# Two mixers of a hybrid diffusion backbone: later gate tiles traced while the pooling is awaited, the decays of both directions in one piece, and other filling steps

## The chip, the cores and the metric

The kernel runs on one core of one Trainium2 chip, as one launch. The metric is the device time of that launch in microseconds (us). The engines that matter here are TensorE (PE, matrix products; its weight loads are shown as PEld), VectorE (DVE), ScalarE (ACT, activation functions and copies), and SyncE (SP), which issues the DMAs. All tensors are fp32 in HBM.

## The reference

Two layers (DEPTH = 2) act on 256 latent tokens and 256 context tokens of width 1024. Each layer is a half-step SwiGLU FFN, a token mixer, and another half-step FFN, all with adaLN shift, scale and gate. The mixer is the part that matters here:

```python
cq, ckv, kr, pz, gq, gk, gv, ga, gr, gates = split_cols(u @ w_in)
q, k, v = mla_project(cq, ckv, kr, ...)      # low-rank q and kv, RMS-norm per head, rotary part
o_a = blocked_attend(q, k_all, v_all)        # 8 heads; latent queries see context and latent keys
o_p = multiscale_pool(pz, w_pool, pool_scale)  # 4 channel groups, windows 2/4/8/16
og  = gla_bidir(qg, kg, vg, la, s_f, s_b)    # gated linear attention, forward and backward scan
o_g = gla_output(og, gr, g_gla_o)            # RMS-norm, times silu(gr)
g = sigmoid(gates)                           # 3 x 1024 gate channels
m = g[0] * (o_a @ w_branch[0]) + g[1] * (o_p @ w_branch[1]) + g[2] * (o_g @ w_branch[2])
y = m @ w_out
```

In GLA every direction has its own decay: `log_sigmoid` of a low-rank product, summed over chunks of 64 tokens, and its exponentials scale queries and keys. The context tokens of the second layer need no mixer output, so mixer 1 computes queries, gates and outputs for the 256 latent tokens alone, and mixer 0 for all 512. Only the latent stream is returned.

## The kernel before

Activations lie transposed, channels on the 128 partitions, tokens along the row (512: latent, then context). Every product with a weight is three fp32r matmuls (mm3, lines 219 to 221) of a high and a low part of both operands. Weights come in 512 KB pieces through SP's queue into four raw buffers. ACT copies out the high part (whi, traced at line 185 by act) and DVE subtracts (wlo, line 197). The class Weights loads and cuts ahead, in the order in which the trace asks for the pieces, as far as the raw buffers and 20 slots of 128x512 (in the mixers) reach. In all there are 71 such slots in SBUF and 8 PSUM banks of 128x512.

A planner schedules what the Python code traces: each engine has one queue, and its order is in the main that of the trace, with single instructions moved by the planner's own times. So the order of tracing is the tuning knob. A mixer is written as generators that are advanced in turn (mixer, lines 665 to 735):

- attend: the set-up of keys and queries (step a0: squares; a1: norms of the compressed q and kv; four steps k: two heads' keys each, with key_tail, the mean and the scaling, one step behind; then the value products, the last key_tail; four steps q: two heads' queries each; qs: the queries' scale rq), then per block scores (s) and turn and value products (t). Scores, row maximum (mx), exponential (p), sum and division run over PE, DVE and ACT, and the turned p goes through PSUM (pt, pT).
- gla: two pairs of heads. gla_prepare makes the logits (line 1157), for each direction the decays (lines 1159 to 1181, Abs, Exp and Ln on ACT, a scan on DVE) with a step g1, and turns the end-scaled keys (ket, line 1186, step g2). gla_pair makes A (line 1207, g3), the state increments ds and the state chain st (lines 1225 to 1233, g3), the outputs o per head (lines 1244 to 1258, g4), and their turn ot (g5).
- pool: for each of the four groups, windowed sums on DVE (line 1109), 1 + POOL[l] steps of waiting, and the product with w_pool, whose result goes to self.op.
- filler: all the remaining PE work, in pieces of half a weight tile (twelve matmuls; tile_of). In mixer 0: four pooling inputs, then a wait for self.op, branch 1 (per four channels: gate tiles 8 to 15 where they are missing, sigmoids, four branch products), the GLA inputs, four output gates (gr), a wait for the attention's outputs self.oa, branch 0, four gate tiles, a wait for GLA, branch 2. In mixer 1 the GLA inputs come first.

In mixer 0 attend and gla run one behind the other, in mixer 1 in turn. After every step of either the pool is advanced by one step, and the filler gets the credit that FILL[l] names for that step; one whole credit is one filler step. A filler step spent while the filler waits for self.op or self.oa emits nothing. What is left of the filler is emitted when both chains have ended. act keeps the order of all users of an activation table: sigmoid and silu need another table than exp and ln, so each change of kind is a table load (line 181) that lies between its users in ACT's queue.

Of the kernel before, what the change touches and what calls it, by code (L numbers as in the profile page):

```python
# [15 lines left out]
P = 128  # L16
# [23 lines left out]
ROOM_0, ROOM_1, LAST = 8, 36, 4  # L40
S0, S1, S2 = 7, 3, 3

FILL = (dict(a0=1.5, a1=2, k=1.5, q=0, qs=2, s=0.5, t=1, g1=3, g2=3.5, g3=1.5, g4=1.5, g5=0, w=0.5),
        dict(a0=1, a1=1.5, k=2, q=3.5, qs=0.5, s=2, t=2, g1=0.5, g2=0, g3=0.5, g4=1, g5=0.5, w=0.5))
POOL = (0, 1)
EDGE = {(1, 17): (1, 2), (0, 17): (0, 2)}
LATE = 100
ADA = dict(up=(1.5, 1.25, 1, 0), down=(1, 1, 1, 0), mix=(12, 10), late=(8, 26), pre=(2, 1, 1, 0), premix=(0, 0))
# [89 lines left out]
class Net:  # L138
# [611 lines left out]
    def filler(self, adas):  # L750


        n, u, l = self.n, self.u, self.l
        w_in = self.a["w_in"][l]
        left = [adas]

        def tile_of(c0, m):
            unit = self.cols(w_in, 0, KD, c0)
            o = self.ps("fill")
            for k in range(KD):  # L760
                self.mm3(o[:, 0:m], unit.block(k), (u[k][0][:, 0:m], u[k][1][:, 0:m]), k == 0, k == KD - 1)
                if k == 3:
                    yield 1
            self.w.done(unit)
            left[0] -= 1
            if 0 <= left[0] < ADA["mix"][l]:
                self.adas(1)
            self.got = o

        def kept(c0, m, name):  # L770
            yield from tile_of(c0, m)
            t = self.slot(name=name, n=m)
            self.act(out=t[:, 0:m], in_=self.got[:, 0:m], func=AF.Copy)
            self.got = t

        def gate(j):
            yield from kept(2496 + j * P, n, "gate")
            self.gates[j] = self.got
            yield 1

        def branch(i, x):
            wb = self.a["w_branch"][l, i]
            for d0 in range(0, KD, 4):
                dcs = range(d0, d0 + 4)
                for dc in dcs:
                    if 8 * i + dc not in self.gates:
                        yield from gate(8 * i + dc)
                for dc in dcs:
                    s = self.gates[8 * i + dc]
                    self.act(out=s[:, 0:n], in_=s[:, 0:n], func=AF.Sigmoid)  # L790
                for dc in dcs:
                    s = self.gates.pop(8 * i + dc)
                    (o,) = self.dense([self.cols(wb, 0, 4, dc * P)], x, n)
                    self.nc.vector.tensor_tensor(out=s[:, 0:n], in0=s[:, 0:n], in1=o[:, 0:n], op=ALU.mult)
                    if dc in self.m:
                        self.nc.vector.tensor_tensor(out=s[:, 0:n], in0=s[:, 0:n], in1=self.m[dc][:, 0:n], op=ALU.add)
                    self.m[dc] = s if i < 2 else self.parts(s[:, 0:n], n)
                    yield 1

        def pools():  # L800
            for g in range(4):
                yield from tile_of(416 + g * P, n)
                self.pz[g] = self.got
                yield 1

        def glas():
            for c0, m, to in ((1184, T, self.gk), (928, n, self.gq)):
                for c in range(2):
                    yield from kept(c0 + c * P, m, "gqk")
                    to.append(self.got)  # L810
                    yield 1
            out = [self.ps("gv") for _ in range(4)]
            for q in range(4):
                unit = self.cols(w_in, 2 * q, 2, 1440, T)
                for kk in range(2):
                    k = 2 * q + kk
                    for tt, o in enumerate(out):
                        x = tuple(t[:, tt * P:(tt + 1) * P] for t in u[k])
                        self.mm3(o, x, unit.block(kk, T), k == 0, k == KD - 1)
                    if kk == 0:  # L820
                        yield 1
                self.w.done(unit)
                if q < 3:
                    yield 1
            for o in out:
                t = self.slot(name="gv")
                self.act(out=t, in_=o, func=AF.Copy)
                self.gv.append(t)
            yield 1

        if not self.full:
            yield from glas()
        yield from pools()
        while len(self.op) < 4:
            yield 1
        yield from branch(1, self.op)
        self.op.clear()
        if self.full:
            yield from glas()
        for g in range(4):  # L840
            yield from kept(1984 + g * P, n, "gr")
            self.gr.append(self.got)
            yield 1
        while len(self.oa) < 4:
            yield 1
        oa = [self.parts(t[:, 0:n], n) for t in self.oa]
        self.oa.clear()
        yield from branch(0, oa)
        oa.clear()
        for dc in range(4):  # L850
            yield from gate(16 + dc)
        while len(self.on) < 4:
            yield 1
        og = []
        for h in range(4):
            self.act(out=self.gr[h][:, 0:n], in_=self.gr[h][:, 0:n], func=AF.Silu)
        for h in range(4):
            t = self.on[h]
            self.nc.vector.tensor_tensor(out=t[:, 0:n], in0=t[:, 0:n], in1=self.gr[h][:, 0:n], op=ALU.mult)
            og.append(self.parts(t[:, 0:n], n))  # L860
        self.on.clear()
        self.gr.clear()
        yield from branch(2, og)


    def attend(self):
        nc, l, n, a = self.nc, self.l, self.n, self.a
# [23 lines left out]
        t = self.slot(name="ckv")  # L891
# [8 lines left out]
        for j, p in enumerate((pq0, pq1)):  # L900
            t = self.slot(name="cq")
# [28 lines left out]
        def key_tail(j, ps, sq):  # L930
            ms = self.ps("kms")
            nc.tensor.matmul(ms, cst[:, C_1H:C_1H + P], sq, start=True, stop=True)
            r = sq
            self.rstd_from(ms, r)
            for x in range(2):
                o = slice(64 * x, 64 * x + 64)
                t = self.slot(name="k")
                nc.vector.scalar_tensor_tensor(out=t[0:64], in0=ps[o], scalar=vec[o, V_KN2:V_KN2 + 1], in1=r[o], op0=ALU.mult, op1=ALU.mult)
                nc.vector.tensor_tensor(out=t[64:128], in0=krr[o], in1=r[o], op=ALU.mult)
                keys[2 * j + x] = t  # L940
# [11 lines left out]
        v = []  # L952
        for tt in range(4):
# [3 lines left out]
            t = self.slot(name="v")  # L957
            self.act(out=t, in_=ps, func=AF.Copy)
            v.append(t)
        self.w.done(wkv)  # L960
        key_tail(*pend)


        wq = []
# [17 lines left out]
        q = []  # L982
# [158 lines left out]
    def gla_prepare(self, c, ready):  # L1141
# [16 lines left out]
        for d, ps in enumerate(logits):  # L1158
            bias = vec[:, V_BA + 2 * d + c:V_BA + 2 * d + c + 1]
            e = self.slot(name="e")  # L1160
            self.act(out=e, in_=ps, func=AF.Abs, bias=bias)
            self.act(out=e, in_=e, func=AF.Exp, scale=-1.0)
            self.act(out=e, in_=e, func=AF.Ln, bias=1.0)
            la = self.slot(name="la")
            nc.vector.tensor_scalar(out=la, in0=ps, scalar1=bias, scalar2=0.0, op0=ALU.add, op1=ALU.min)
            nc.vector.tensor_tensor(out=la, in0=la, in1=e, op=ALU.subtract)
            b = self.slot(name="b")
            if d == 0:
                nc.vector.tensor_tensor_scan(out=b, data0=rst, data1=la, initial=0.0, op0=ALU.mult, op1=ALU.add)
            else:  # L1170
                nc.vector.tensor_tensor_scan(out=b[:, ::-1], data0=rst, data1=la[:, ::-1], initial=0.0, op0=ALU.mult, op1=ALU.add)
            end = 63 if d == 0 else 0
            nc.vector.tensor_tensor(out=chunk(la), in0=chunk(b)[:, :, end:end + 1].to_broadcast([P, 8, 64]), in1=chunk(b), op=ALU.subtract)
            self.act(out=la, in_=la, func=AF.Exp, scale=1.0 / 16)
            nc.vector.tensor_tensor(out=la, in0=gk, in1=la, op=ALU.mult)
            ket.append(la)
            self.act(out=e, in_=b, func=AF.Exp, scale=1.0 / 16)
            self.act(out=b[:, 0:n], in_=b[:, 0:n], func=AF.Exp, scale=-1.0 / 16)
            nc.vector.scalar_tensor_tensor(out=qt[d][:, 0:n], in0=gq[:, 0:n], scalar=0.125, in1=e[:, 0:n], op0=ALU.mult, op1=ALU.mult)
            nc.vector.tensor_tensor(out=kt[d][:, 0:n], in0=gk[:, 0:n], in1=b[:, 0:n], op=ALU.mult)  # L1180
            nc.vector.tensor_copy(dec[:, d, :], chunk(e)[:, :, end])
            yield "g1"
        for d in range(2):
            pt = self.ps("ket")
            for tt in range(4):
# [209 lines left out]
```

## Time and profile before

| | |
|---|---|
| median of 3 runs | 2154.8 us (2153.69 to 2155.99) |
| the profiled execution's own time | 2152.27 us |
| its span in the profile | 2150.5 us |
| mean granted PE clock | 0.983 |
| HBM traffic | 287.44 MB read, 134 GB/s over the span |
| mixer 0, from its norm to its last output tile | about 421 to 897 us |
| mixer 1, likewise | about 1644 to 1946 us |

A row of a timeline reads: start, duration (us), engine, line, operation, output <- inputs, form, count, and in brackets the idle time of that engine just before and what ended it. A matmul's duration includes its pipeline, so back-to-back matmuls start closer together than they last. A stretch's clock of 0.58 means that PE got 58% of its full clock on average. Names are the kernel's tile names; fill is a filler tile in PSUM, ps any dense product, uhi and ulo the normed input.

### The profile page before, as it was taken

To read this page: it belongs to the slowest core of one execution; us is meant where nothing else is said; L and a number is where in the kernel's file an instruction comes from. 1 tells how busy PE (TensorE), PEld (TensorE's weight loads), DVE (VectorE), ACT (ScalarE), POOL (GpSimd) and SP (SyncE) were. 2 spreads that over 40 slices of the span, in tenths; PEclk is the share of its full clock that TensorE was granted. 3 is DMA by queue.
4 is the path that set the end of the run, shared out by engine and by line. 5 is a ranking of instruction groups with operands and counts; after the bars stand their busy time and mean duration, and the time that the engine had idled before them with its cause. 6 is when DMAs were issued, how large, how long until landed. Compare 5 with 4: busy or idle time off the path is not lost.

```text
span 2150.5 us, 29894 instructions
## 1 busy us (share of the span) xinstructions
PE 2084.2 (97%) x11388; PEld 1752.5 (81%) x11388; DVE 1453.7 (68%) x2870; ACT 882.3 (41%) x1797; POOL 2.0 (0%) x10
## 2 busy tenths in 40 slices
PE   7999999898999999999999989999999998999999
PEld 4888778786777887888888888888888777998997
DVE  4577877867586665666876785767544687666564
ACT  5232223455344555433223342323343656665552
POOL 0000000000000000000000000000000000000000
PEclk9999999999999999999999999999999989999999
DMA  9355554514432223445555453546442332566663
GB/s 318 100 152 157 172 166 134 160 39 127 118 108 69 79 69 98 119 124 152 164 164 161 135 149 102 151 141 186 137 115 59 96 101 80 142 163 192 181 197 127
DMA packets 431071, 290.43 MB, mean 135 GB/s; under 512 B 16464, under 2 KB 386768, under 8 KB 430928
## 3 DMA queue, kind: packets, MB, share of 16 engines
q1 hardware_dynamic: 430016, 287.09, 46.6%
q8 instruction: 89, 1.46, 0.3%
q10 hardware_dynamic: 912, 1.44, 0.2%
q14 instruction: 54, 0.44, 0.1%
HBM read 287.44 MB, written 1.05 MB: 134 GB/s over the span
## 4 chain that ended last, share of the span: by engine, by line
PE 74%; DVE 11%; DMA 9%; ACT 3%; issue 2%; ACTq 0%; SPq 0%; DVEq 0%
PE ps L219 17%; PE ps L220 17%; PE ps L221 17%; DMA raw<-in_ffn_w_dram 9%; PE fill L219 4%; PE fill L221 4%; PE fill L220 4%; DVE wlo L197 4%; DVE adaacc L358 2%; ACT whi L185 2%; PE sc L1031 1%; PE av L1067 1%; PE ada L327 1%; PE pt L1049 1%; PE gv L219 1%
## 5 line engine op out<-in xcount | busy, mean ns | idle before, releaser
L197 DVE TENSOR_TENSOR wlo<-raw,whi 128x512 fp32r<-128x512 f32 (+3 forms) x912 | 531.3, 619 | 290.0 <-ACT whi L185 279.6
L185 ACT ACTIVATE whi<-raw 128x512 fp32r<-128x512 f32 (+3 forms) x912 | 471.9, 568 | 521.5 <-DMA raw<-in_ffn_w_dram 469.8
L219 PE MATMUL ps<-uhi,whi 128*128 128x512 f32 (+1 forms) x1620 | 564.3, 350 | 8.7 <-ACT uhi L185 5.1
L221 PE MATMUL ps<-uhi,wlo 128*128 128x512 f32 (+1 forms) x1620 | 561.8, 348 | 1.1 <-DVE wlo L197 1.1
L220 PE MATMUL ps<-ulo,whi 128*128 128x512 f32 (+1 forms) x1620 | 562.3, 348 | 0.0
L219 PEld LDWEIGHTS ps<-uhi,whi 128*128 128x128 f32 x1620 | 308.0, 191 | 53.7 <-ACT uhi L185 8.7
L221 PEld LDWEIGHTS ps<-uhi,wlo 128*128 128x128 f32 x1620 | 308.8, 191 | 41.3 <-DVE wlo L197 3.6
L220 PEld LDWEIGHTS ps<-ulo,whi 128*128 128x128 f32 x1620 | 309.3, 191 | 37.9 <-DVE ulo L475 0.6
L358 DVE SCALAR_TENSOR_TENSOR adaacc<-raw,csil,adaacc 128x512 f32<-128x512 f32 x420 | 294.6, 744 | 1.6 <-DMA raw<-in_w_ada_dram 0.8
L219 PE MATMUL ps<-hi,whi 128*128 128x512 f32 (+1 forms) x738 | 272.8, 371 | 6.9 <-DVE h L501 5.4
L221 PE MATMUL ps<-hi,wlo 128*128 128x512 f32 (+1 forms) x738 | 272.0, 369 | 0.2 <-DVE wlo L197 0.2
L220 PE MATMUL ps<-lo,whi 128*128 128x512 f32 (+1 forms) x738 | 271.5, 368 | 0.0
L219 PE MATMUL fill<-uhi,whi 128*128 128x512 f32 (+1 forms) x576 | 203.9, 354 | 0.0
L221 PE MATMUL fill<-uhi,wlo 128*128 128x512 f32 (+1 forms) x576 | 195.9, 340 | 0.0
L220 PE MATMUL fill<-ulo,whi 128*128 128x512 f32 (+1 forms) x576 | 195.4, 339 | 0.0
L219 PEld LDWEIGHTS ps<-hi,whi 128*128 128x128 f32 x738 | 141.2, 191 | 29.8 <-DVE h L501 5.8
L221 PEld LDWEIGHTS ps<-hi,wlo 128*128 128x128 f32 x738 | 141.2, 191 | 23.2 <-DVE wlo L197 0.6
L220 PEld LDWEIGHTS ps<-lo,whi 128*128 128x128 f32 x738 | 141.3, 192 | 22.4 <-DVE lo L197 0.2
L570 DVE TENSOR_TENSOR silu<-silu,ps 128x512 f32<-128x512 f32 (+1 forms) x88 | 54.2, 616 | 133.7 <-ACT silu L185 79.3
L185 ACT ACTIVATE silu<-ps 128x512 f32<-128x512 f32 (+1 forms) x88 | 47.4, 539 | 195.4 <-PE ps L221 195.1
L219 PEld LDWEIGHTS fill<-uhi,whi 128*128 128x128 f32 x576 | 109.3, 190 | 21.7 <-issue 10.6
L220 PEld LDWEIGHTS fill<-ulo,whi 128*128 128x128 f32 x576 | 109.4, 190 | 13.5 <-issue 2.4
(265 smaller groups left out, 2192.0 us busy)
## 6 DMA issues: line engine op xcount, KB each, us to landing
raw<-in_ffn_w_dram SPq DMA_DIRECT2D x198, 512.0 KB, 4.4
raw<-in_w_ada_dram SPq DMA_DIRECT2D x128, 512.0 KB, 3.8
raw<-in_w_in_dram SPq DMA_DIRECT2D x86, 512.0 KB, 4.4
raw<-in_ffn_w_dram SPq DMA_DIRECT2D x48, 384.0 KB, 3.9
raw<-in_ffn_w_dram SPq DMA_DIRECT2D x48, 320.0 KB, 3.2
raw<-in_w_branch_dram SPq DMA_DIRECT2D x48, 256.0 KB, 2.9
ada<-in_w_ada_dram SPq DMA_DIRECT2D x32, 256.0 KB, 5.4
raw<-in_w_out_dram SPq DMA_DIRECT2D x16, 512.0 KB, 5.0
```

The lines of the kernel that those rows point to most:

```text
L185: i = self.nc.scalar.activation(**k)
L197: self.nc.vector.tensor_tensor(out=lo, in0=src, in1=f32hi, op=ALU.subtract)
L219: mm(out, wh, xh, start=start, stop=False)
L220: mm(out, wh, xl, start=False, stop=False)
L221: mm(out, wl, xh, start=False, stop=stop)
L327: nc.tensor.matmul(ps[32 * g:32 * g + 32, :], self.csil[:, k, :], r[i], start=(k < 4), stop=(k >= 4))
L358: nc.vector.scalar_tensor_tensor(out=acc[s], in0=r[i], scalar=c, in1=acc[s], op0=ALU.mult, op1=ALU.add)
L570: nc.vector.tensor_tensor(out=s[:, 0:n], in0=s[:, 0:n], in1=p3[:, 0:n], op=ALU.mult)
L1031: nc.tensor.matmul(sc[:, 0:nk], q[h][:, tt * P:(tt + 1) * P], keys[h][:, k0:T], start=True, stop=True)
L1049: nc.tensor.transpose(pt[:, (2 * x + j) * P:(2 * x + j + 1) * P], ps_[j][:, (kt + x) * P:(kt + x + 1) * P], self.ident)
L1067: nc.tensor.matmul(av[0][64 * x:64 * x + 64, s * NL:(s + 1) * NL], v[2 * s + kt][:, (h + x) * 64:(h + x) * 64 + 64], pts[x][kt // 2][:, (k ...
```

## The change

Four edits, all in the order of the trace:

- The filler, while self.op is awaited, traces up to GATES[l] later tiles (2 in mixer 0; 12 in mixer 1) where it traced nothing: first the gates 8 to 15, then the output gates gr. What is made there is left out where it stood.
- attend has two new steps "v", before and after the last key_tail, with one credit each in mixer 0 and none in mixer 1 (where each step also gives gla and the pool their turn).
- gla_prepare traces the decays of both directions in one piece and then yields g1 twice.
- Credits change: in mixer 0 q from 0 to 0.5; in mixer 1 qs from 0.5 to 1.5, g1 from 0.5 to 1.5, g3 from 0.5 to 1. POOL[0] goes from 0 to 1, so the pool of mixer 0 waits one more step between a group's sums and its product.

```diff
--- before.py
+++ after.py
@@ -40,9 +40,10 @@
 ROOM_0, ROOM_1, LAST = 8, 36, 4
 S0, S1, S2 = 7, 3, 3
 
-FILL = (dict(a0=1.5, a1=2, k=1.5, q=0, qs=2, s=0.5, t=1, g1=3, g2=3.5, g3=1.5, g4=1.5, g5=0, w=0.5),
-        dict(a0=1, a1=1.5, k=2, q=3.5, qs=0.5, s=2, t=2, g1=0.5, g2=0, g3=0.5, g4=1, g5=0.5, w=0.5))
-POOL = (0, 1)
+FILL = (dict(a0=1.5, a1=2, k=1.5, v=1, q=0.5, qs=2, s=0.5, t=1, g1=3, g2=3.5, g3=1.5, g4=1.5, g5=0, w=0.5),
+        dict(a0=1, a1=1.5, k=2, v=0, q=3.5, qs=1.5, s=2, t=2, g1=1.5, g2=0, g3=1, g4=1, g5=0.5, w=0.5))
+POOL = (1, 1)
+GATES = (2, 12)
 EDGE = {(1, 17): (1, 2), (0, 17): (0, 2)}
 LATE = 100
 ADA = dict(up=(1.5, 1.25, 1, 0), down=(1, 1, 1, 0), mix=(12, 10), late=(8, 26), pre=(2, 1, 1, 0), premix=(0, 0))
@@ -773,6 +774,11 @@
             self.act(out=t[:, 0:m], in_=self.got[:, 0:m], func=AF.Copy)
             self.got = t
 
+        def out_gate(g):
+            yield from kept(1984 + g * P, n, "gr")
+            self.gr.append(self.got)
+            yield 1
+
         def gate(j):
             yield from kept(2496 + j * P, n, "gate")
             self.gates[j] = self.got
@@ -831,16 +837,21 @@
         if not self.full:
             yield from glas()
         yield from pools()
+
+        later = [gate(8 + j) for j in range(8)] + [out_gate(g) for g in range(4)]
+        spare = GATES[l]
         while len(self.op) < 4:
-            yield 1
+            if spare:
+                spare -= 1
+                yield from later.pop(0)
+            else:
+                yield 1
         yield from branch(1, self.op)
         self.op.clear()
         if self.full:
             yield from glas()
-        for g in range(4):
-            yield from kept(1984 + g * P, n, "gr")
-            self.gr.append(self.got)
-            yield 1
+        for g in range(len(self.gr), 4):
+            yield from out_gate(g)
         while len(self.oa) < 4:
             yield 1
         oa = [self.parts(t[:, 0:n], n) for t in self.oa]
@@ -958,7 +969,9 @@
             self.act(out=t, in_=ps, func=AF.Copy)
             v.append(t)
         self.w.done(wkv)
+        yield "v"
         key_tail(*pend)
+        yield "v"
 
 
         wq = []
@@ -1179,7 +1192,8 @@
             nc.vector.scalar_tensor_tensor(out=qt[d][:, 0:n], in0=gq[:, 0:n], scalar=0.125, in1=e[:, 0:n], op0=ALU.mult, op1=ALU.mult)
             nc.vector.tensor_tensor(out=kt[d][:, 0:n], in0=gk[:, 0:n], in1=b[:, 0:n], op=ALU.mult)
             nc.vector.tensor_copy(dec[:, d, :], chunk(e)[:, :, end])
-            yield "g1"
+        yield "g1"
+        yield "g1"
         for d in range(2):
             pt = self.ps("ket")
             for tt in range(4):
```

## The prediction

> **What bounds the kernel now.** I read the page first, then the busy time by stretches, the waits of TensorE (PE) in the two mixers, and last the timelines around the longest waits.
>
> ```profile
> span 2150.5 us, 29894 instructions
> PE 2084.2 (97%) x11388; PEld 1752.5 (81%) x11388; DVE 1453.7 (68%) x2870; ACT 882.3 (41%) x1797; POOL 2.0 (0%) x10
> ```
>
> PE is busy in 97% of the span, so a change that moves work without removing any can win only where PE stands idle or runs below its full clock. The stretches show where that is. Columns: stretch, its length, busy time of PE, PE's weight loads, DVE, ACT and POOL with instruction counts, the granted PE clock, DMA share, GB/s.
>
> ```profile
> 480.00:520.00 40.00, 33.04 (x140) 24.02 (x139) 31.37 (x62) 24.44 (x52) 0.00 (x0) 0.87 0.33 92
> 1718.00:1853.70 135.70, 122.36 (x960) 100.72 (x959) 104.86 (x248) 83.80 (x184) 0.00 (x0) 0.91 0.33 87
> 1718.00:1744.80 26.80, 26.60 (x241) 22.08 (x240) 24.18 (x60) 18.61 (x44) 0.00 (x0) 1.00 0.36 94
> 1744.80:1761.10 16.30, 11.24 (x50) 6.92 (x50) 12.96 (x41) 5.04 (x14) 0.00 (x0) 0.58 0.16 48
> 1785.90:1798.60 12.70, 4.62 (x23) 3.49 (x24) 9.70 (x21) 9.25 (x18) 0.00 (x0) 0.60 0.21 61
> 1853.70:1917.30 63.60, 63.60 (x529) 63.52 (x530) 42.04 (x81) 41.63 (x91) 0.00 (x0) 1.00 0.69 183
> ```
>
> The first row is the query stage of mixer 0, the second the whole attention and GLA stage of mixer 1 with its two bad places below it. The last row is the rest of mixer 1's filler, made when both chains have ended: PE is full there. So any filler tile made earlier, in an idle place, shortens that stretch one for one. The waits (waiting line, what it waited for, total us, times, longest), the first four from mixer 0, the others from mixer 1:
>
> ```profile
> PE pool L219 <- ACT hi L185: 3.8, 1, 3.8
> PE kms L932 <- DVE k L938: 2.4, 1, 2.4
> PE q L219 <- ACT sqk L185: 0.8, 1, 0.8
> ...
> PE o L1248 <- DVE st L1233: 0.5, 1, 0.5
> ...
> PE ket L1186 <- DVE la L1175: 8.3, 2, 8.1
> PE pool L219 <- ACT hilo L185: 2.3, 2, 1.8
> PE o L1244 <- DVE op L1128: 1.7, 1, 1.7
> PE o L1248 <- DVE st L1233: 1.1, 1, 1.1
> ```
>
> **The most the change can win.** Idle time plus the part of the busy time that the clock withheld. Mixer 0: 40.00 - 33.04 = 6.96 us idle, which is the first three waits (7.0); the clock took (1 - 0.87) x 33.04 = 4.3. Together 11.3. Mixer 1, around 1745: 16.30 - 11.24 = 5.06 idle, and 0.42 x 11.24 = 4.7 by the clock; around 1786: 12.70 - 4.62 = 8.08 idle, and 0.40 x 4.62 = 1.9. Together 19.7. The cap is 31.0 us.
>
> **The change, part by part.** No arithmetic is added or removed: two yields are new, and the order changes. I counted the steps of both mixers by the code, since each yield gives the filler its credit. A filler step is twelve matmuls:
>
> ```profile
> 447.37:450.12 2.75, 2.75 (x15) 2.26 (x14) 0.49 (x1) 2.22 (x5) 0.00 (x0) 1.00 0.00 0
> ...
> 1717.48 0.28 PE L219 MATMUL fill<-uhi,whi 128*128 128x256 f32 x1
> ...
> 1718.80 0.28 PE L221 MATMUL fill<-uhi,wlo 128*128 128x256 f32 x1
> ```
>
> The first row is one step of mixer 0 (2.75 us). The other two start the first and the twelfth matmul of a step in mixer 1: 1.32 us for eleven gaps, so 0.12 us each and 1.44 us a step.
>
> *Decays in one piece (mixer 1).* The 8.1 us wait has a plain cause in the timelines of ACT and PE:
>
> ```profile
> 1781.66 1.28 ACT L181 ACT_TABLE_LOAD   x1
> ...
> 1783.45 1.33 ACT L185 ACTIVATE gate<-gate 128x256 f32<-128x256 f32 x4
> ...
> 1785.31 1.28 ACT L181 ACT_TABLE_LOAD   x1
> ...
> 1787.14 0.67 ACT L185 ACTIVATE e<-logit,vec 128x512 f32<-128x512 f32 x1
> ```
>
> ```profile
> 1719.01 1.13 PE L1157 MATMUL logit<-ga,wa 32*128 32x512 f32 x4
> ...
> 1734.67 0.55 PE L1186 MATMUL ket<-cst,la 128*128 128x128 f32 x3 [0.20 <-DVE la L1175]
> ...
> 1774.44 1.13 PE L1157 MATMUL logit<-ga,wa 32*128 32x512 f32 x4
> ...
> 1794.02 1.11 PE L1186 MATMUL ket<-cst,la 128*128 128x128 f32 x4 [8.09 <-DVE la L1175]
> ```
>
> The second fence has the two pairs of GLA heads, each from its logits to its ket. In the second both logits were there at 1775.6, but a yield lies between the two directions, the filler put four gate sigmoids into it, and act() keeps the order of table users. So the second direction began at 1787.14, behind two table loads. After the change both decays are traced before any filler, and by my count no sigmoid falls between them in either pair. Seven filler steps, a score block and a turn lie between logits and ket of the second pair, about 12.5 us, where both decays took 14.5 us in the first pair (1720.1 to 1734.7), with a filler step between them. I expect this wait to go, or to shrink to 0 to 2 us.
>
> *Gates while the pooling is awaited (mixer 1).* Twelve filler steps are empty now between the pooling's first group and its fourth, in exactly the 1745 stretch. Afterwards none is: gates 8 to 15 fill them, and the pooling, decay and state steps get 1.4 to 5.8 us of cover each. The extra weight cuts meet a DVE that is 90% busy just before (24.18 of 26.80). The state updates after ds still need DVE. I leave 3 us of wait here (bounds 0 and the 5.06 idle of now).
>
> *What is late next.* The filler is finite. Four output gates and the eight gates are made early, then the filler waits for all of the attention's output: four empty steps now, 24 afterwards. From the second pair's A products on (scores 4 to 7, both halves of o, the last turns) there is no cover at all. PE work of that stage, from the same stage of before, which ran full; the second and third rows are its filler tiles and branch products:
>
> ```profile
> 1799.55:1853.69 54.14, 54.14 (x463) 46.02 (x461) 37.70 (x87) 32.27 (x69) 0.00 (x0) 1.00 0.33 89
> 1799.55:1853.69 54.14, 26.37 (x193) 23.89 (x193) 3.02 (x8) 1.00 0.33 89
> 1799.55:1853.69 54.14, 6.82 (x48) 5.98 (x48) 1.59 (x4) 0.00 (x0) 1.00 0.33 89
> ```
>
> 54.14 - 240 x 0.12 = 25.3 us, in 18 pieces of 1.4 us on average. Its DVE and ACT work:
>
> ```profile
> L197 DVE TENSOR_TENSOR wlo<-raw,whi 128x512 fp32r<-128x512 f32 x19 | 12.5, 686 | 7.4 <-ACT whi L185 7.3
> L1033 DVE TENSOR_REDUCE mx<-sc 128x1 f32<-128x512 f32 x8 | 5.5, 689 | 2.8 <-PE sc L1031 2.8
> L1039 DVE TENSOR_SCALAR p<-p,mx 128x512 f32<-128x512 f32 x8 | 3.9, 487 | 0.3
> L1233 DVE SCALAR_TENSOR_TENSOR st<-st,dec,ds 128x128 f32<-128x128 f32 x12 | 3.9, 344 | 0.2
> L1054 DVE COPY pT<-pt 128x512 f32<-128x512 f32 x5 | 3.4, 685 | 1.5 <-PE pt L1049 1.5
> ...
> L185 ACT ACTIVATE p<-sc,mx,scal 128x512 f32<-128x512 f32 x16 | 12.4, 774 | 10.7 <-DVE mx L1035 10.7
> ```
>
> DVE without the weight cuts: 37.70 - 12.5 = 25.2, as much as PE, so latency decides. The o products need fourteen state updates (14 x 0.34 = 4.8) behind two score maxima (1.4): 6.2, against a turn and the first o products, some 2 us: 4.2 short. A score block's softmax takes 0.69 + 0.77 + 0.49 and some small ones, 2.3 for its first half and about 3.5 for both. The last two turns have two pieces of cover each (2.8): 0.7 short twice, and the last copy (0.69) before the last products. Sum 6.3. A wait of that size is followed by a low clock: two such drops cost 4.3 us in mixer 0, so 2.1 for one. I take 8.4. Bounds: 0 if the planner puts gate tiles from behind into the gaps (it does move single matmuls, as the pooling product amid the ds shows), and at the other end the 1745 stretch, which ran like operations without cover: 0.58 x 11.24 = 6.5 us of full-clock work in 16.30, a factor 2.5, +38 us here.
>
> ```profile
> 1739.86 0.39 PE L219 MATMUL pool<-hilo,whi 128*128 128x256 f32 x1
> 1740.17 0.65 PE L1225 MATMUL ds<-gv,ket 64*64 64x128 f32 x10
> ```
>
> The clock has a page in the Trainium skill, "TensorE: Matmul & The Clock Gate", section "HAM oscillation — how this bites in real kernels": only idle gaps beyond some 3.4 us cost clock. By that rule the late stage's short gaps would keep it, save perhaps the 4.2, and its loss would be 6.3 rather than 8.4. The 1745 stretch disagrees: its gaps are 1.7, 1.1 and 1.8 us, and its clock 0.58.
>
> *The middle of that stage* (from the branch products to the second ket) has both sigmoid batches and the cuts for five more weight tiles. DVE's 104.86 us are then 91% of a stage of 115. I take 3 us of waits, bounds 0 and 6.
>
> Mixer 1: -19.7 + 3 + 3 + 8.4 = -5.3.
>
> *Mixer 0.* The new steps at "v" put gate 8 between the value products and the last keys' mean, and gate 9 around the first queries, two steps of 2.75 us against waits of 2.4 and 0.8. The pooling's third group gets a step of fill and two query steps before its product, where it had one query step: the 3.8 us go. But POOL[0] = 1 moves the fourth group's product past the query stage. Its sums are then traced behind the last query, and only qsum and the turn of rq (about 1.5 us) lie before its product; three steps there are empty, as GATES[0] = 2 is spent. The chain is seven operations of about 0.7 on DVE and ACT, 5 us by these rows:
>
> ```profile
> 499.76 0.72 DVE L1109 TENSOR_TENSOR poolsum<-zp 128x542 f32<-128x542 f32 x1
> ...
> 508.01 0.63 ACT L185 ACTIVATE hi<-pooled 128x512 fp32r<-128x512 f32 x1 [1.65 <-DVE pooled L1115]
> ```
>
> 5 - 1.5 = 3.5 us of new wait (bounds 0, and 8.9 - 1.5 = 7.4 if it takes as long as it did here, from 499.76 to 508.64). With 0.5 for what is left of the first two, mixer 0 gives -11.3 + 4 = -7.3. The two gates' weight loads go ahead of the query weights in SP's queue; DMA is 33% busy there, so this costs nothing, and at most one tile's cut (1.4 us of DVE) if that cover is gone. In the GLA stage of mixer 0 PE waited 0.5 us at most (the fourth row of the waits), and the one-piece decays change nothing there.
>
> **Sum.** -5.3 - 7.3 = -12.6 against the profiled execution's 2152.27 us: 2139.7. The median of the runs, 2154.8, stands 2.5 above it: 2142.
>
> **Rivals.** (A) *Everything hides.* The planner fills the late stage and the fourth pooling group, and little over 3 us of the 31 stays: 2127. For it: PE full after 1853.7, with tiles ready to be pulled forward. Against: at 1786 it pulled none.
> (B) *The gaps only move.* DVE sets the stage: 104.86 in 135.70 is 77%, and if it can't do better, mixer 1 gains nothing, and mixer 0 what is left beside a fourth-group wait of 7.4, some 4 us: 2151. For it: DVE at 90% before 1745. Against: 1718 to 1744.8 shows that 90% can be had.
> (C) *The dry stage costs more than it gave: slower.* If the waits from A to the last av keep PE at half clock throughout, 25.3 us become 50.6, with the 6.3 of waits +31.6 in place of 8.4: 2142 + 23 = 2165. It decides once the stage takes 25.3 + 8.4 + 12.6 = 46 us or more, an efficiency under 55%. For it: the 0.40 of the 1745 stretch. Against: there DVE also carried the pooling and a queue of weight cuts, which are done by then.
>
> **How the numbers follow.** Forecast 0.50, A 0.22, B 0.16, C 0.12. No change is 0.2%, 4.3 us either way, which is about what a measurement of this kernel can tell. Forecast and A are faster but for 0.03 of the forecast's tail, and a third of B is: 0.75. Same: that tail and the rest of B, 0.13. Slower: C, 0.12. The range runs from 2124, all but the whole cap, to 2160, between the forecast's unknowns and C; the forecast's own is 2134 to 2152.
>
> **What would show it.** Right: no ket wait over 2 us; mixer 1's low clock gone before the second A, and back, if at all, behind it; o waiting on st in the second pair; in mixer 0 the kms wait gone and one pool wait of 2 to 5 us just before the gates. Wrong: a ket wait that stays (the sigmoids were not its cause), waits that stand where they stood, or a late stage of over 46 us.

## The result and the profile after

| | before | after |
|---|---|---|
| median of 4 runs each | 2155.14 us (2153.69 to 2155.99) | 2140.12 us (2138.56 to 2142.75) |
| the profiled execution's own time | 2152.27 us | 2142.75 us |
| its span in the profile | 2150.5 us | 2141.0 us |
| mean granted PE clock | 0.983 | 0.987 |

After takes 0.9932 of the time of before (95% interval 0.9915 to 0.9949): 15.0 us by the medians. The two profiled executions differ by 9.5 us only: that of before lies below the runs of the table, that of after is the highest of its four. So terms are measured below in two ways: within the traces, and by runs with one half of the change.

The page of after: the work is the same. Of the 9.5 us of span PE's busy time gives 3.8 (2084.2 - 2080.4) and its idle time the other 5.7.

```profile
PE 2080.4 (97%) x11388; PEld 1750.3 (82%) x11388; DVE 1452.0 (68%) x2870; ACT 883.3 (41%) x1797; POOL 2.0 (0%) x10
```

Where the 9.5 us lie is read from the products of the norm's mean (ms), one ahead of each mixer and one behind it; "from norm to norm" below is the time between their starts. First before, then after, as the timelines of PE have them (start, duration, line):

```profile
420.87 0.60 PE L464 MATMUL ms<-acc,cst 128*128 128x256 f32 x2
...
898.93 0.67 PE L464 MATMUL ms<-acc,cst 128*128 128x256 f32 x2 [2.15 <-DVE acc L448]
...
1644.03 0.59 PE L464 MATMUL ms<-acc,cst 128*128 128x256 f32 x2
...
1948.90 1.22 PE L464 MATMUL ms<-acc,cst 128*128 128x256 f32 x2 [2.73 <-DVE acc L448]
```

```profile
421.79 0.60 PE L465 MATMUL ms<-acc,cst 128*128 128x256 f32 x2
...
896.44 2.06 PE L465 MATMUL ms<-acc,cst 128*128 128x256 f32 x4 [2.15 <-DVE acc L449]
...
1640.90 0.59 PE L465 MATMUL ms<-acc,cst 128*128 128x256 f32 x2
...
1938.47 1.22 PE L465 MATMUL ms<-acc,cst 128*128 128x256 f32 x2 [2.67 <-DVE acc L449]
```

Mixer 0 goes from 478.1 to 474.7 (-3.4), mixer 1 from 304.9 to 297.6 (-7.3), and all the rest together differs by 1.2. Now the stretches of after, cut where its own stages lie: the query stage of mixer 0, then mixer 1's front in two parts, its middle up to the second A products, its late stage up to the last av, and the filler that is left. Columns are those of the prediction's table.

```profile
480.00:520.00 40.00, 36.18 (x167) 26.96 (x166) 32.63 (x71) 25.18 (x60) 0.00 (x0) 0.97 0.25 65
1720.00:1745.00 25.00, 21.03 (x156) 20.06 (x156) 20.20 (x43) 14.71 (x32) 0.00 (x0) 0.86 0.27 71
1745.00:1764.00 19.00, 18.74 (x195) 16.80 (x193) 14.55 (x38) 12.21 (x28) 0.00 (x0) 1.00 0.66 179
1764.00:1813.35 49.35, 47.65 (x365) 41.38 (x366) 42.25 (x97) 38.06 (x81) 0.00 (x0) 1.00 0.43 113
1813.35:1844.00 30.65, 27.79 (x228) 17.75 (x227) 24.18 (x68) 16.60 (x41) 0.00 (x0) 1.00 0.07 20
```

The two bad places of before, clocks of 0.58 and 0.60, are gone. What is late instead stands in the waits of PE, first those of mixer 0, then those of mixer 1 (waiting line, what it waited for, total us, times, longest):

```profile
PE rq L1030 <- ACT rq L186: 3.1, 1, 3.1
PE pt L1062 <- DVE p L1052: 1.5, 1, 1.5
PE q L222 <- DVE wlo L198: 0.7, 1, 0.7
...
PE fill L220 <- ACT whi L186: 4.0, 1, 4.0
PE ot L1278 <- DVE mx L1048: 1.7, 1, 1.7
PE o L1262 <- DVE st L1247: 1.2, 1, 1.2
...
PE ket L1200 <- DVE pT L1067: 0.5, 1, 0.5
```

The waits for the last keys' mean and for the pooling in mixer 0 are gone, and no ket wait is over 0.5. Two waits are new and large. The larger is explained by the timelines of PE and ACT in mixer 1's front:

```profile
1726.98 0.28 PE L222 MATMUL fill<-uhi,wlo 128*128 128x256 f32 x1
1731.23 0.58 PE L220 MATMUL fill<-uhi,whi 128*128 128x256 f32 x1 [3.97 <-ACT whi L186]
```


```profile
1719.90 0.69 ACT L186 ACTIVATE e<-logit,vec 128x512 f32<-128x512 f32 x1 [0.67 <-PE logit L1170]
...
1724.07 0.63 ACT L186 ACTIVATE e<-b 128x512 f32<-128x512 f32 x1 [2.14 <-DVE b L1182]
...
1729.72 0.63 ACT L186 ACTIVATE e<-b 128x512 f32<-128x512 f32 x1 [2.15 <-DVE b L1184]
...
1730.56 0.61 ACT L186 ACTIVATE whi<-raw 128x512 fp32r<-128x512 f32 x1
```

Both directions' decays now follow one another in ACT's queue from 1719.9 on, and ACT stands twice among them for DVE's scan, 2.14 and 2.15 us. The next weight tile's high part is cut behind the second of these stands, at 1730.56, so the filler that should cover the decays runs out of cut tiles after 1726.98 + 0.28 and stands 3.97 us. The other new wait, in mixer 0, has the same form. The next fence is ACT again:

```profile
514.72 0.63 ACT L186 ACTIVATE hi<-pooled 128x512 fp32r<-128x512 f32 x1 [1.81 <-DVE pooled L1128]
515.26 0.67 ACT L186 ACTIVATE rq<-qsum,eps 128x512 f32<-128x512 f32 x1
...
516.35 0.71 ACT L186 ACTIVATE rq<-rq,eps 128x512 f32<-128x512 f32 x1
```

The fourth pooling group's copy waits 1.81 us for DVE and stands ahead of the queries' scale rq in ACT's queue. PE's next product is the one that turns rq, and it waits 3.10 us, until 517.11. The clock was low behind that wait:

```profile
517.00:527.00 10.00, 9.89 (x39) 8.09 (x40) 6.93 (x12) 7.21 (x13) 0.00 (x0) 0.83 0.76 219
```

### The profile page after: what moved, and what is told of

It reads as the page before. It is cut to its first block, busy times and chain, and to the rows that moved or that the text cites. A ratio compares the mean times of both kernels' runs of the same rounds, so it can differ in the third digit from the quotient of the medians.

```text
span 2141.0 us, 29897 instructions
## 1 busy us (share of the span) xinstructions
PE 2080.4 (97%) x11388; PEld 1750.3 (82%) x11388; DVE 1452.0 (68%) x2870; ACT 883.3 (41%) x1797; POOL 2.0 (0%) x10
## 3 DMA queue, kind: packets, MB, share of 16 engines
q10 hardware_dynamic: 912, 1.44, 0.2%
## 4 chain that ended last, share of the span: by engine, by line
PE 76%; DVE 10%; DMA 8%; ACT 4%; issue 2%; ACTq 0%; SPq 0%; DVEq 0%
PE ps L220 18%; PE ps L221 18%; PE ps L222 18%; DMA raw<-in_ffn_w_dram 7%; PE fill L220 4%; PE fill L222 4%; PE fill L221 4%; DVE wlo L198 3%; DVE adaacc L359 2%; ACT whi L186 2%; DMA raw<-in_w_in_dram 1%; PE sc L1044 1%; PE ada L328 1%; PE av L1080 1%; PE gv L220 1%
## 5 line engine op out<-in xcount | busy, mean ns | idle before, releaser
L198 DVE TENSOR_TENSOR wlo<-raw,whi 128x512 fp32r<-128x512 f32 (+4 forms) x912 | 532.2, 619 | 284.4 <-ACT whi L186 271.6
L186 ACT ACTIVATE whi<-raw 128x512 fp32r<-128x512 f32 (+4 forms) x912 | 472.8, 568 | 529.3 <-DMA raw<-in_ffn_w_dram 474.7
```

Of the source, the lines that this page charges most:

```text
L186: i = self.nc.scalar.activation(**k)
L198: self.nc.vector.tensor_tensor(out=lo, in0=src, in1=f32hi, op=ALU.subtract)
```

## The experiments

The runs went in three groups, and each group shares runs of the kernel before (medians 2153.20, 2154.79 and 2155.65). Each ratio, with its 95% interval, is an estimate over the runs of its group and not the quotient of the two medians; in e1 the two differ most. Microseconds given with a ratio are worked out from it. Diffs are against after, unless one says otherwise.

**Only mixer 1's part (e1).** The v steps and the one-piece decays apply to mixer 1 alone.

```diff
-FILL = (dict(..., v=1, q=0.5, ...), ...)
-POOL = (1, 1)
-GATES = (2, 12)
+FILL = (dict(..., v=0, q=0, ...), ...)
+POOL = (0, 1)
+GATES = (0, 12)
```

> Only the edits that act in mixer 1 (12 early tiles, one-piece decays, its credits, its two v steps); mixer 0 as before. If the two mixers' gains are separate, as the prediction summed them, this gives the mixer 1 share: the traces of before and after show mixer 1 shorter by 7.3 us from norm to norm, so about 2147 to 2148, and mixer 0 keeps its waits of 2.4, 0.8 and 3.8 us. If mixer 0's edits did nothing (its new 3.1 us wait ate what the old ones cost), the time is the changed kernel's own, 2140.

Measured: 2146.51 us, 0.9957 (0.9944 to 0.9969). In microseconds the ratio is -9.3 (-12.1 to -6.7); the medians lie 6.7 apart. Mixer 0 keeps its three waits of before (3.7, 2.4 and 0.8 here), and mixer 1 has the filler's wait of 4.0 as in after.

**Only mixer 0's part (e2).** The converse.

```diff
-        dict(..., qs=1.5, ..., g1=1.5, g2=0, g3=1, ...))
-GATES = (2, 12)
+        dict(..., qs=0.5, ..., g1=0.5, g2=0, g3=0.5, ...))
+GATES = (2, 0)
...
-        yield "v"
+        if l == 0:
+            yield "v"
```

> Only the edits that act in mixer 0 (2 early gates, POOL 1, v steps, q credit, one-piece decays); mixer 1 as before. Separate gains: 3.4 us by the traces, up to the 7.3 of the prediction, so 2148 to 2152, with the ket wait of 8.1 us in mixer 1 still there and a wait of about 3 us on rq in mixer 0. If mixer 0's edits did nothing: 2155.

Measured: 2148.87 us, 0.998 (0.9971 to 0.999), or -4.3 us (-6.2 to -2.2). By the ratios the two halves add up: 0.9957 x 0.998 = 0.9937, against 0.9932 for the whole. By the medians they give 6.7 + 4.3 = 11.0 of 15.0 us, which the intervals also allow. In the waits of e2, mixer 0 has the rq wait of after, and mixer 1 the ket wait of before:

```profile
PE rq L1032 <- ACT rq L186: 3.1, 1, 3.1
...
PE ket L1205 <- DVE la L1190: 8.8, 2, 8.4
```

**Only the decays in one piece (e3).** Before, with nothing but the moved yield:

```diff
--- before
             nc.vector.tensor_copy(dec[:, d, :], chunk(e)[:, :, end])
-            yield "g1"
+        yield "g1"
+        yield "g1"
```

> The kernel before with the decays of both directions in one piece and nothing else (same credits, same steps). My theory: the 8.1 us wait of ket goes, since no sigmoid lies between the two directions, which is worth 8.1 of idle time and 1.9 of clock, less a new wait for weights whose cuts now stand behind both decays in ACT's queue (4.0 idle and 2.6 of clock in the changed kernel): 2145 to 2152. Rival, the gaps only move: the ket wait turns up as another wait of the same size, 2153 to 2157.

Measured: 2150.37 us, 0.9984 (0.9975 to 0.9992), -3.4 us. In the waits of mixer 1 the 8.1 has become 2.7, and a filler tile waits for its cut:

```profile
PE ket L1187 <- DVE la L1175: 2.7, 1, 2.7
PE fill L221 <- DVE wlo L197: 1.5, 1, 1.5
```

**All but the one piece (e4).**

```diff
             nc.vector.tensor_copy(dec[:, d, :], chunk(e)[:, :, end])
-        yield "g1"
-        yield "g1"
+            yield "g1"
```

> The changed kernel with the decays split again (a step between the directions, the same two g1 credits). My theory is that ket waited for sigmoids between the directions and not for the split itself. By the count of steps the early gates have moved both batches of sigmoids away from there, so ket waits under 2 us here too, the wait of 4.0 us for the cut weights goes, and the time is 2134 to 2140. Rival: the split itself costs the wait (two decays one behind the other with a step between), ket waits some 8 us again, and the time is 2148 or more.

Measured: 2139.26 us, 0.9927 (0.9915 to 0.9939), the same as the whole change. Beside the early gates the one piece is worth nothing that these times can show. The split brings a ket wait of 3.3, more than the 2 that was expected, and halves the filler's wait:

```profile
PE ket L1199 <- DVE la L1188: 3.3, 1, 3.3
...
PE fill L220 <- ACT whi L186: 1.9, 2, 1.4
```

And the sigmoids are no longer between the directions though these are split, as ACT's timeline shows for the second pair: the last table load ends before the first direction's decay starts, and none follows until the second's, at 1796.38.

```profile
1783.31 1.28 ACT L182 ACT_TABLE_LOAD   x1
...
1787.69 0.68 ACT L186 ACTIVATE e<-logit,vec 128x512 f32<-128x512 f32 x1
```

**The sigmoids alone (e5).** Before, with one empty filler step ahead of branch 1's first sigmoids, so that they fall behind the second direction:

```diff
--- before
                         yield from gate(8 * i + dc)
+                if l == 1 and i == 1 and d0 == 0:
+                    yield 1
                 for dc in dcs:
```

> The kernel before with one thing moved: in mixer 1 the filler spends one more step before the first four sigmoids of branch 1, so that they fall behind the second direction's decay; the decays stay split. My theory (the second decay waited behind the sigmoids and their two table loads): ket waits about 3 us instead of 8.1, as it did with split decays in the changed kernel, and the time falls by 4 to 7 us, to 2146 to 2150. Rival: DVE or the missing cover made the wait, ket still waits 7 us or more and the time stays within 2 us of 2153.

Measured: 2151.67 us, 0.9985 (0.9977 to 0.9994), -3.2 us: less than expected, and the ket wait is 5.5, between the theory's 3 and the rival's 7. The second pair in its timelines, ACT and then PE, to be held against the rows of before in the prediction:

```profile
1774.78 0.69 ACT L185 ACTIVATE e<-logit,vec 128x512 f32<-128x512 f32 x1
1780.93 0.68 ACT L185 ACTIVATE e<-logit,vec 128x512 f32<-128x512 f32 x1
```

```profile
1773.02 1.13 PE L1159 MATMUL logit<-ga,wa 32*128 32x512 f32 x4
...
1788.59 1.11 PE L1188 MATMUL ket<-cst,la 128*128 128x128 f32 x4 [5.51 <-DVE la L1177]
```

The table loads now come behind, and the second direction starts 6.15 us after the first, where it was 11.25 (1787.14 - 1775.89). But from the logits to the second ket it takes 15.57, against 19.58 before (1794.02 - 1774.44): 4.0 less. The moved step took 1.44 us of cover away, and 8.09 - 4.0 + 1.44 = 5.5 is the wait that is left. So the sigmoids were half of the 8.1, 4.0 with the cover unchanged. The other half, by elimination, is that two directions in series take longer than what is traced beside them.

**No early gates (e6).**

```diff
-GATES = (2, 12)
+GATES = (0, 0)
```

> The changed kernel without early gate tiles (GATES 0 and 0): the steps while the pooling is awaited are empty again in both mixers, all other edits stay. My theory: the early gates are what fills the 1745 stretch; without them mixer 1 has waits of 4 to 6 us and a low clock there again, gains back the 2 to 4 us of the uncovered late stage, and mixer 0 has its waits around the last keys' mean again: 2145 to 2150. Rival: the one-piece decays and the credits are the gain and the gates only move work: 2139 to 2142.

Measured: 2160.92 us, 1.0036 (1.0023 to 1.005): slower than before by 7.8 us (5.0 to 10.8) by the ratio. Both the theory (2145 to 2150) and its rival (2139 to 2142) missed this. The moved decays and the new credits stay, and the credits are spent on empty steps. Waits of mixer 1:

```profile
PE pool L220 <- ACT hilo L186: 5.1, 2, 3.5
PE fill L220 <- ACT whi L186: 4.0, 1, 4.0
```

The pooling wait of before (2.3) is back and larger, and the filler's wait behind the decays stays. In mixer 0 the wait at rq is 4.5 us, where after has 3.1. So the gates in the empty steps carry the gain; without them the rest of the change costs time. Which part of the rest costs it (credits, the v steps, POOL[0], the one piece) was not run one by one.

**Cover for rq (e7).** Four early tiles in mixer 0 instead of two, so that PE has work while the fourth pooling group holds rq.

```diff
-GATES = (2, 12)
+GATES = (4, 12)
```

> The changed kernel with GATES 4 and 12: mixer 0 makes four gates early, so the three steps that are empty around qsum get a tile. My theory: the 3.1 us wait of rq in mixer 0 (its activation stands behind the fourth group's pooled split in ACT's queue, and PE has nothing before it) is covered, which is worth 3.1 of idle and about 1 of clock: 2135 to 2138. Rival: the wait moves to the fourth pooling product or to slots that the two more gates hold, 2139 to 2143.

Measured: 2135.36 us, 0.9914 (0.9901 to 0.9928). The product that turns rq starts without a wait, at 520.90, and the stretch around it is full and has its clock:

```profile
520.90 0.60 PE L1030 MATMUL rq<-cst,rq 128*128 128x128 f32 x4
...
500.00:530.00 30.00, 30.00 (x137) 22.41 (x136) 21.87 (x39) 18.13 (x32) 0.00 (x0) 1.00 0.42 122
```

**Room to cut ahead (e8).** Four more slots for cut weights in mixer 1, so that tiles are cut before ACT goes into the decays.

```diff
-        self.w.room = ROOM_MIX
+        self.w.room = ROOM_MIX if full else ROOM_MIX + 4
```

> The changed kernel with 24 instead of 20 slots of cut weights in mixer 1, one tile more ahead. My theory: the new 4.0 us wait of a filler tile on its cut (ACT) comes because the cut is traced behind both decays and ACT stands 2.1 us twice for DVE's scans before it; one tile more ahead puts the cut before the decays, the wait and its low clock (4.0 + 2.6) go: 2133 to 2136. Rival: ACT and DVE are simply full there, and a wait of 3 to 4 us stays somewhere between the logits and ket: 2138 to 2142.

Measured: 2135.95 us, 0.9917 (0.9904 to 0.9931). ACT still stands for the second scan as in after, 2.15 us, but the filler's wait of 4.0 is gone and the front has its clock; 1.8 us is left there, a pooling product's wait for its own weight's cut (ACT's timeline, then the stretch):

```profile
1727.88 0.63 ACT L186 ACTIVATE e<-b 128x512 f32<-128x512 f32 x1 [2.15 <-DVE b L1184]
```

```profile
1720.00:1745.00 25.00, 23.22 (x196) 22.47 (x196) 22.31 (x50) 16.96 (x40) 0.00 (x0) 1.00 0.42 113
```

So that wait came from when the tile was cut, not from how long the decays take.

**Both (e9), gates in the late stage too (e10), interleaved decays (e11), split decays (e12).** e9 has the edits of e7 and e8. e10 adds gates 0 to 7, which nothing holds, while mixer 1 waits for the attention's output: this fills the late stage.

```diff
+        later = [gate(j) for j in range(8)]
         while len(self.oa) < 4:
-            yield 1
+            if later and not self.full:
+                yield from later.pop(0)
+            else:
+                yield 1
```

e11 adds to e10 that the two directions' decays are traced in three steps, each for both directions: the logits' logarithm, the scan, the exponentials. e12 adds to e10 the split of e4. The core of e11:

```diff
             nc.vector.tensor_tensor(out=la, in0=la, in1=e, op=ALU.subtract)
+            es.append(e)
+            las.append(la)
+        for d in range(2):
+            la = las[d]
             b = self.slot(name="b")
...
+            bs.append(b)
+        for d in range(2):
+            e, la, b = es[d], las[d], bs[d]
             self.act(out=la, in_=la, func=AF.Exp, scale=1.0 / 16)
```

> The changed kernel with both single repairs, GATES 4 and 12 and 24 slots of cut weights in mixer 1. The two waits lie in different mixers, so if each repair took away a wait of its own the gains add: ratios 0.9914 and 0.9917 against 0.9932 of the changed kernel give 0.990, about 2133. Rival: both only profit from the same luck of the clock, 0.991 to 0.992.

> The kernel with both repairs, and in mixer 1 the gates 0 to 7 of branch 0 are made while the attention's outputs are awaited, so that the late stage, dry in the changed kernel, has 16 filler steps. The late stage's price by the prediction was 8.4 us, by the trace of the changed kernel 2.9 to 4.1 us of idle time with no low clock. If the trace is right, 2 to 4 us less than with the two repairs alone; by the prediction's figure 6 to 8 us less; if the more cuts on DVE and ACT make the late stage longer, no gain or a loss.

> The same as the kernel with gates in the late stage, and in addition the two decays of a pair are traced interleaved (both absolute values, exponentials and logarithms, then both scans, then the rest), so that ACT does not stand twice for DVE's scan. If ACT's standing order is what the cuts and ket waited for, the last ket and cut waits (1 to 3 us) go; if not, the time is the same within 1.5 us.

> The same as the kernel with gates in the late stage, but with the decays split again by a step. In the changed kernel split and one-piece decays gave the same time (0.9927 and 0.9932). With its cut wait repaired the one-piece form should now be ahead by about the ket wait of the split form, 2 to 3 us; if the decays' form is worth nothing beside the gates, the times agree within 1.5 us.

| | median us | ratio | interval |
|---|---|---|---|
| e9 both | 2128.42 | 0.9874 | 0.9857 to 0.9890 |
| e10 with late gates | 2127.98 | 0.9873 | 0.9859 to 0.9888 |
| e11 interleaved | 2124.31 | 0.9857 | 0.9842 to 0.9872 |
| e12 split | 2129.16 | 0.9877 | 0.9862 to 0.9891 |

e9 is 11.7 us under after by the medians; 4.8 (e7) and 4.2 (e8) would have given 9.0, and the intervals allow that. The ratio is lower than the expected 0.990, and the rival of e9 (0.991 to 0.992) is out. All four beat both kernels. e10 against e9 is not decided by the times: 0.4 us, where each interval is some 3 us either way. In the traces the late stage of e9 stands 3.00 us in 55, and that of e10 0.08 (first e9, then e10):

```profile
1800.00:1855.00 55.00, 52.00 (x430) 41.97 (x430) 39.00 (x94) 30.93 (x72) 0.00 (x0) 1.00 0.41 106
```

```profile
1800.00:1855.00 55.00, 54.92 (x467) 45.63 (x465) 41.01 (x96) 35.64 (x84) 0.00 (x0) 1.00 0.41 110
```

From norm to norm mixer 1 takes 293.18 us in e9 (1631.53 to 1924.71) and 288.74 in e10 (1635.49 to 1924.23), 4.4 less. The whole executions hide it: e10's reached mixer 0 at 423.52 and e9's at 419.67, though their code is the same up to mixer 1. So by one trace each, what is left dry there is worth 3 to 4 us; the times do not show it.

e11 is the fastest of all, but its interval overlaps those of e9, e10 and e12; that interleaving helps is not shown. ACT's four waits for DVE among the first pair's decays come to 2.1 us (1.04, 0.55, 0.20 and 0.28) where e10 has 2.08 and 2.15, but the pooling product's wait stays (1.9 against 1.8), and mixer 1 is only 0.7 us shorter from norm to norm than in e10. e12 against e10 is not decided by the times either (1.2 us). In its trace a ket wait of 3.0 is back, and mixer 1 takes 291.94 from norm to norm, 3.2 more than in e10: what the expectation gave to the one piece once its cut wait is repaired. That is one execution each.

## Why the prediction was right, and where its terms were not

The forecast was 2142 and the median is 2140.1, inside the forecast's own range; faster was right, and none of the rivals came about. The mechanism held: idle places were filled, and what was taken from the late filler did not cost more than it gave. But the terms were off in both directions, and they partly cancelled.

- *The sum.* Predicted -12.6, of it mixer 1 -5.3 and mixer 0 -7.3. The halves measured alone gave -9.3 (-12.1 to -6.7, e1) and -4.3 (-6.2 to -2.2, e2): both predicted terms lie outside, mixer 1's gain too low and mixer 0's too high. Traces of other runs, which share one mixer's code with before or after, say the same from norm to norm. Mixer 0 takes 478.06, 479.66 and 477.75 with the code of before (before, e1, e5) and 474.65, 471.68 and 472.02 with that of after (after, e2, e8): -5.7 by the means. Mixer 1 takes 304.87 and 306.98 (before, e2) and 297.57, 297.74 and 296.96 (after, e1, e7): -8.5. Together that is -14.2, close to the 15.0 of the medians; the trace of after alone has an untypically long mixer 0. So the total came out nearly right in part by luck: errors of some 3 and 2 us had opposite signs.
- *The dry late stage* is the term that was mis-sized most: 8.4 predicted, 2.9 measured (30.65 - 27.79, at full clock). The waits for the state updates (4.2 predicted) measured 1.2, the turns' 1.7. PE was busy for 27.8 us there, where I had counted 25.3 without any filler; the planner pulled 1.0 us of filler into it (the row below: that stretch, filler tiles alone, in after), so the reason given for the lower bound, that the planner fills the gaps, hardly counts, and the chain itself was shorter than its parts had suggested. Filling the stage in e10 shortened mixer 1 by 4.4 in the trace, still half of 8.4. Rival C, at half clock throughout, needed 46 us, and the stage took 30.65.

```profile
1813.35:1844.00 30.65, 1.00 (x6) 0.82 (x7) 0.00 (x0) 1.00 0.07 20
```

- *The front of mixer 1* measured more than the 3 us left for it: 3.97 + 0.26 idle, and 0.14 x 21.03 = 2.9 by the clock, 7.2 in all, above the bound of 5.06, which had left the clock out. The step that failed is that I looked at DVE's load alone ("extra weight cuts meet a DVE that is 90% busy") and costed the decays' moved yield as a gain only. The edit puts a chain with two stalls ahead of a cut in ACT's queue. e8 shows that: with the tiles cut earlier the wait is gone, and the scans take what they took.
- *The middle*: 49.35 - 47.65 = 1.7, predicted 3. Together mixer 1 gives -19.7 + 7.2 + 1.7 + 2.9 = -7.9 by its stages; in this pair of traces it has -7.3 from norm to norm.
- *The 8.1 us ket wait* went, as predicted, but the cause was only half right. e5 takes the sigmoids away and 5.5 stays; e3 takes the split away and 2.7 stays; e4 keeps the split and still has 3.3, because the early gates had moved the sigmoids already. The prediction credited the one-piece decays with the whole of it. In the change as made they are worth nothing that the times show; e6 shows that the early gates carry the gain.
- *Mixer 0*: the kms and pooling waits went, as predicted, and q waits 0.7 for a weight cut. The new wait was foreseen in place and size, 3.5 against 3.10, but it stands one product earlier, at rq: I counted rq's turn as cover of the pooling chain, and it lies behind that chain in ACT's queue. In the stage the idle time fell to 3.82, and the clock behind the rq wait took 0.17 x 9.89 = 1.7: -11.3 + 5.5 = -5.8, as the traces of the several runs have it (-5.7). It falls short of -7.3 by the clock, which the predicted 3.5 had left out. From norm to norm after's own trace has -3.4 only. The rest is seen elsewhere in that mixer: its first 9 us ran at a clock of 0.81 (rows in the last section), 0.19 x 6.57 = 1.2, and one turn of the scores (pt) waits 1.5, where e2's waits 0.3.
- *What would show it.* No ket wait over 2: seen. The low clock gone before the second A: seen from 1745 on, but a new one stands in the 25 us ahead of that. o waiting on st in the second pair: seen, 1.2. One pooling wait of 2 to 5 before the gates: seen as the rq wait.

The 1745 stretch of before and the late stage of after have gaps of one size and opposite clocks. First the gaps of before's stretch, then those of after's late stage, 12 us apart and with a clock of 1.00, both from PE's timeline:

```profile
1746.49 0.71 PE L1244 MATMUL o<-gv,Asum 128*128 128x128 f32 x4 [1.67 <-DVE op L1128]
...
1748.31 0.69 PE L1248 MATMUL o<-st,qt 64*64 64x128 f32 x2 [1.11 <-DVE st L1233]
...
1750.83 0.58 PE L219 MATMUL pool<-hilo,whi 128*128 128x256 f32 x1 [1.84 <-ACT hilo L185]
```

```profile
1821.30 0.43 PE L1262 MATMUL o<-st,qt 64*64 64x128 f32 x2 [1.17 <-DVE st L1247]
...
1833.22 0.41 PE L1278 MATMUL ot<-cst,sqo 128*128 128x128 f32 x2 [1.70 <-DVE mx L1048]
```

In before the three gaps stood within 6 us, and the clock fell to 0.58. The Trainium skill ("TensorE: Matmul & The Clock Gate", section "HAM oscillation — how this bites in real kernels") has low clock follow idle gaps beyond some 3.4 us. The late stage agrees with it (longest gap 1.70, clock 1.00), and the prediction would have done better to follow it there: by it that stage cost 6.3, not 8.4, still twice what was measured. The 3.97 us gap of after, with 0.86 over its 25 us, agrees too. The 1745 stretch does not, and the rq wait, 3.10 us, lies just below the rule's figure and has 0.83 over the 10 us behind it. That short gaps close together count as one would fit both stretches, but no run here tests it, and the last section has equal gaps with two different clocks.

## What to carry to other kernels

When work is traced in one piece, look at what stands behind it in each in-order queue: a chain that waits for another engine holds back unrelated preparations (here weight cuts and a scale) that PE needs, and here room to prepare further ahead (e8), or two more tiles of cover (e7), removed that. The gain came from the empty steps of the filler: without the early gates the rest of the change was slower than before. Work taken from a full stage behind may cost less there than the dry stage's own chain suggests (2.9 us of waits here for 8.4 expected). Before crediting an edit with a wait, ask whether the other edits of the change move the same wait away.

## What the runs showed of the hardware

The clock differs between executions where the work does not. Mixer 0 has the same code in before and in e1, and in both traces the gaps of PE at its start are 1.09 and 0.96 us. The first 9 us of it, before and then e1, and as a third row after, whose gaps there are 1.47 and 0.96:

```profile
420.87:429.87 9.00, 6.95 (x53) 6.17 (x52) 8.08 (x21) 6.16 (x15) 0.00 (x0) 1.00 0.16 41
...
419.31:428.31 9.00, 6.95 (x40) 6.17 (x39) 8.17 (x22) 6.14 (x15) 0.00 (x0) 0.81 0.23 60
...
421.00:430.00 9.00, 6.57 (x38) 5.80 (x37) 8.17 (x21) 5.97 (x14) 0.00 (x0) 0.81 0.34 100
```

With equal gaps the clocks are 1.00 and 0.81, and the rows count 53 and 40 matmuls in the same 6.95 us of busy time; 0.19 x 6.95 = 1.3 us is the clock's. So the sizes of the gaps do not decide the clock alone, and a difference of 1 to 2 us between two profiled executions can be the clock's. A term of that size needs repeated runs, or several traces that share the code in question, as in the sum above.
